# Bias tiles with buffers of their own, loaded in an earlier feed-forward instead of in attention

## The chip, the cores and the metric

The kernel runs on one core of a Trainium2 chip. The metric is the device time of one execution in microseconds (us); the runs of a kernel are given by their median. The profile is of one execution on that core. Its engines are PE (matrix products; PEld is its weight load), DVE (vector), ACT (activations and copies), POOL (a slower vector engine) and SP, whose queue issues the DMAs of this kernel. Each engine works through its own queue in order and waits for others by semaphores.

## The reference

Two layers over 256 positions of width 1024, in float32. A layer is a half-step SwiGLU feed-forward, a mixer, and another half-step feed-forward, each behind an RMS norm. Layer 0's mixer is a gated short convolution; layer 1's is a sparse attention with 16 heads in 4 groups, whose keys and values were computed from layer 0's output.

```python
for i in range(DEPTH):
    if i == N_A_LAYERS:
        kv = shared_kv(h, kv_norm, w_kv, k_norm, ...)
    h = h + 0.5 * swiglu_ffn(rmsnorm(h, ffn1_norm[i]), ffn1_w_in[i], ffn1_w_out[i])
    hn = rmsnorm(h, mix_norm[i])
    if i < N_A_LAYERS:
        h = h + short_conv_mixer(hn, conv_w_in[i], conv_w[i], conv_w_out[i])
    else:
        h = h + nsa_mixer(hn, attn_w_q[j], attn_q_norm[j], attn_w_o[j], rel_bias, kv)
    h = h + 0.5 * swiglu_ffn(rmsnorm(h, ffn2_norm[i]), ffn2_w_in[i], ffn2_w_out[i])
...
def head_bias(rel):                      # added to the scores of every branch of the attention
    return rel_bias[rel_bucket(rel)].reshape(rel.shape + (G, HG)).transpose(2, 3, 0, 1)
```

What matters here is the last piece: the bias of a score depends on the head and on the distance of query and key alone, through a table of 32 buckets.

## The kernel before, in words

The residual stream stays in SBUF, transposed (`hall`: 8 tiles of 128 features x 256 positions). Every product is made in split precision: a float32 operand becomes a rounded high part and a low part, and PE multiplies high by high and low, and low by high. Weights come from HBM through one stream `W`. A DMA brings a chunk of 128 x 2048 into one of three `ws` buffers. A chunk is two units of 1024 columns. `W.high()` makes the high half `wh` of a unit on ACT (L145), `W.low()` the low half `wl` on DVE (L162); there are six buffers of each. The DMA of a chunk waits until DVE has read the chunk that had its `ws` buffer before, three chunks earlier. The chunk of the gate weights is narrower and goes through L140 and L157.

A feed-forward (`ffn_in`) takes 22 steps of 16 + 16 matmuls (L321, L324). After each, ACT and DVE evaluate the previous step's gate and prepare the next units, and a function `bg(f)` may add work at step f. In layer 0's second feed-forward there is none.

The bias of the attention is made once: `tables()`, run at the start of that feed-forward, forms for every head a row of minus the bias by distance and writes the 16 rows to a buffer `row_d` in HBM (L259). A bias tile `bias[j]` of 128 x 2 x 256 holds, for two heads, the row shifted by one element per partition. It is read back from `row_d` by a DMA with overlapping rows (`load_bias`, L818). There are eight, one for each j. On POOL, `c_bias` copies every sixteenth column of a tile into `cbias`, for the compressed branch (L823, L824).

Attention is written out as a list of words (`ORDER`) that is worked through from left to right, each word adding instructions to the queues of one or more engines. The words that matter: `LB_j` loads a bias tile and `CBI_j` copies from it; `WA_u` and `WD_u` are one `W.high()` and one `W.low()`; `F` is six matmuls of the later queries (L900 to L902); `qs`, `qr`, `root`, `recip`, `qn` are the norm of the first queries (ACT L838, DVE L843 and L847, ACT L850, DVE L854 and L873); `GT`, `GC`, `GA`, `GX`, `GE`, `GD` are the gates (PE L915, ACT L920, DVE L923, PE L928, ACT L934, DVE L938 on); `QT` and `QC` transpose the queries and apply their gain (PE L884, ACT L888); `S_j` are the scores of heads j (PE L956), `M` their minima with the bias added (DVE L964; L968 for the compressed branch, from `cbias`), `E` the exponentials (ACT L975), `R` the reciprocals (DVE L979), `N` the scaling (on POOL L990 and L993). Ahead of the list four bias tiles are loaded, and the first queries' product (`b_full`, L584 to L586) is made, with the sums of squares in its middle (`q_mid`, L831). The tiles `act` are a ring of 22 buffers of 128 x 512, used for the feed-forward's hidden tiles, for the bias tiles, and for the attention's transposed queries, weights and outputs. A bias load waits until the last reader of its `act` buffer is done.

Of the kernel before, what the change touches and what calls it, by code (L numbers as in the profile page):

```python
# [9 lines left out]
F32 = mybir.dt.float32  # L10
# [6 lines left out]
P = 128  # L17
# [8 lines left out]
OHW = 512  # L26
# [11 lines left out]


ORDER = """  # L40
CBI_0 GT WA_0 CBI_3 CBI_1 LB_7 qs_0 LB_5 WD_0 LB_4 LB_6 CBI_2 qs_1 F GC qr_0 WA_1 F qr_1 F GA F root exp recip qn_0 GX
F qn_1 GE WD_1 QT_0 QT_1 QC_0 F GD QC_1 S_0 F M_0_1 F F M_0_0 SQ_2 F E_0_1 CBI_4 RD_2 S_1 CBI_5 CBI_7 NW_2 E_0_0 CBI_6
F F F WA_2 QM_2 F R_0_0 WA_3 R_0_1 N_0_0 M_1_1 QT_2 F QC_2 F M_1_0 E_1_1 N_0_1 T_0_0 CM_0 S_2 C_0_0_d SQ_3 R_1_1 WD_2
E_1_0 N_1_1 T_0_1 M_2_1 H_0 CH_0 R_1_0 E_2_1 M_2_0 CX_0 T_1_1 N_1_0 RD_3 S_3 E_2_0 R_2_1 NW_3 N_2_1 T_1_0 CE_0 C_1_1
C_0_1 H_1 M_3_1 C_1_0 CH_1 T_2_1 C_2_1 R_2_0 M_3_0 N_2_0 E_3_1 CR_0 S_4 CM_1 QM_3 E_3_0 CG_0 R_3_1 WD_3 T_2_0 N_3_1
H_2 QT_3 CI_0 M_4_0 QC_3 C_2_0 R_3_0 CL_0 M_4_1 T_3_1 E_4_0 CX_1 CP_0 N_3_0 CPC_0_d S_5 CE_1 R_4_0 E_4_1 CR_1 C_3_1_d
V_1 CG_1 M_5_0 N_4_0 CI_1 CH_2 T_3_0 R_4_1 M_5_1 E_5_0 V_0 CL_1 CM_2 C_3_0_d N_4_1 E_5_1 T_4_0 R_5_0 S_6 C_4_0_d O_0
R_5_1 CP_1 O_1 CX_2 P_0 T_4_1 N_5_0 P_1 CE_2 H_4 CPC_1 CR_2 H_3 M_6_0 CH_4 V_2 CH_3 C_4_1 M_6_1 CG_2 E_6_0 V_3 N_5_1
CI_2 S_7 R_6_0 O_2 O_3 CL_2 P_2 E_6_1 N_6_0 P_3 CP_2 M_7_1 T_5_1 T_5_0 CPC_2 H_5 C_5_1_d C_5_0 V_4 R_6_1 CH_5_d E_7_1
N_6_1 M_7_0 T_6_0 V_5 O_4 R_7_1 CM_3 E_7_0 P_4 CX_3 N_7_1_d WO_0_a O_5 C_6_0 R_7_0 P_5 N_7_0 WA_4 WO_1_a WA_5 WD_4  # L50
T_6_1 CE_3 WD_5 T_7_0 C_6_1 H_6 C_7_0 WO_2_a CH_6_d CR_3 CG_3 WO_3_a CI_3 CL_3 CP_3 T_7_1 CPC_3 H_7 C_7_1_d V_6 CH_7
V_7 O_6 P_6 WO_1_b O_7 P_7 WO_3_b WO_0_b WO_2_b WO_2_c WO_0_c WO_3_c WO_1_c
"""


# [1 line left out]
def trunk(ctx, tc, A, out):  # L57
    nc = tc.nc
    ve, ac, pe, po, sy = nc.vector, nc.scalar, nc.tensor, nc.gpsimd, nc.sync
# [9 lines left out]
    def mk(shape, tag, bufs, dt=F32, pool=None):  # L69
        uid[0] += 1  # L70
        return (pool or sb).tile(list(shape), dt, tag=tag, name=f"{tag}_{uid[0]}", bufs=bufs)

    def one(shape, name, dt=F32):
        return cp.tile(list(shape), dt, tag=name, name=name)
# [4 lines left out]
    def bank2():  # L79
        return mk([P, 2, 512], "mm", 2, pool=ps)  # L80

    def act(shape=(P, 512), dt=F32R):
        return mk(shape, "act", 22, dt)
# [161 lines left out]
    row_d = dr.tile([16, OHW], F32, tag="row", name="row_d")  # L245
# [16 lines left out]
    def new_xs():  # L262
        return [mk([P, 512], "xs", 8, F32R) for _ in range(8)]
# [66 lines left out]
    def total(o, n):  # L330

        r = t2([P, n, T])
        ac.copy(r, o[:, :, T:])  # L333
        ve.tensor_tensor(out=r, in0=o[:, :, :T], in1=r, op=ALU.add)  # L334
        return r
# [4 lines left out]
    def weave(gen):  # L340
        for _ in gen:
            W.pump(1)
        W.pump()

    def ffn_evac(r, R, hid):
        times(r, R, 2)
        yield
        s = t1()
        ac.activation(s, r[:, 0], AF.Silu)  # L349
        ve.tensor_tensor(out=s, in0=s, in1=r[:, 1], op=ALU.mult)  # L350
        yield
        hd = act()
        split(s, hd)
        hid.append(hd)

    def a_group(parts, xs, mid=None):
        us = W.take(len(parts))
        if mid is None:
            a_pass([(o, u, xs, range(8)) for o, u in zip(parts, us)])
        else:  # L360
            a_pass([(o, u, xs, range(6)) for o, u in zip(parts, us)])
            a_pass([(o, u, xs, [6]) for o, u in zip(parts, us)])
            mid()
            a_pass([(o, u, xs, [7]) for o, u in zip(parts, us)])
        W.done(len(parts), False)

    def ffn_in(xs, norm, R=None, bg=None, pre=None, sums=(), rms=None):

        hid, sums = [], list(sums)
        box = [R]  # L370
        n0 = len(sums)

        def mid():
            if pre is not None:
                pre()
            box[0] = norm.rows()

        for f in range(n0, NF):
            o = bank2()
            if f == n0 and n0:  # L380
                box[0] = rms(o)
            else:
                a_group([o[:, 0], o[:, 1]], xs, mid if f == 0 and R is None else None)
            sums.append(total(o, 2))
            for _ in range(2 if len(sums) > 1 else 1):
                weave(ffn_evac(sums.pop(0), box[0], hid))
            if bg is not None:
                bg(f)
        return hid
# [55 lines left out]
    xs = new_xs()  # L445
    nm = Norm([(xs, G_FFN1)])
# [69 lines left out]
    hid = ffn_in(xs, nm, sums=first_tiles(), rms=first_rms)  # L516
    xs = new_xs()
    nm = Norm([(xs, G_MIX)])
# [39 lines left out]
    xs = new_xs()  # L558
    nm = Norm([(xs, G_FFN2)])
    tab = tables()  # L560
    next(tab)
    out_proj(zs, 1.0, nm)
    hid = ffn_in(xs, nm, pre=lambda: list(tab))


    xs = new_xs()
    xk_a = mk([P, 4, 512], "kt", 1, F32R)
    xkv = [xk_a[:, k] for k in range(4)] + [t2(dt=F32R) for _ in range(4)]
    nm = Norm([(xkv, G_KV), (xs, G_FFN1 + 8)])
# [72 lines left out]
    for tt in range(2):  # L642
        for x in range(2):
            src = oc[tt][:, x * 256:(x + 1) * 256].rearrange("p (a d) -> p a d", d=64)
# [115 lines left out]
    def bg(f):  # L760

        if f == 0:
            kv["s"] = squares(kns)
        elif f == 1:
            r = inv_rms(kv["s"])
            for tt in range(2):
                v = kns[tt].rearrange("p (n d) -> p n d", d=64)
                po.tensor_tensor(out=v, in0=v, in1=r[:, tt * 8:tt * 8 + 8, None].to_broadcast([P, 8, 64]), op=ALU.mult)
        elif f in (2, 3, 4, 5):
            c_trans((f - 2) % 2, (f - 2) // 2)  # L770
        elif f in (6, 7):
            k_trans(f - 6)
        elif f == 8:
            po.tensor_tensor(out=both, in0=ident[:, :64], in1=ident[:, 64:], op=ALU.add)
            po.tensor_tensor(out=both48, in0=ident[:96, :48], in1=ident[:96, 48:96], op=ALU.add)
        elif f == 9:
            kv["rk"] = rh_split(0)
        elif f == W1AT[0]:
            kv["ak"] = c_hidden(kv["rk"])
        elif f == 12:  # L780
            kv["ak"] = c_total(kv["ak"])
            kv["rv"] = rh_split(1)
            W.limit = NBUF
        elif f == W1AT[1]:
            kv["av"] = c_hidden(kv["rv"])
            kv["kc"] = kc_norm(c_second(kv["ak"], 0))
        elif f == 15:
            kv["av"] = c_total(kv["av"])
        elif f == 16:
            kc_trans(kv["kc"])  # L790
        elif f == 17:
            c_values(kv["av"])

    hid = ffn_in(xs, None, R1, bg)
    xs = new_xs()
    nm = Norm([(xs, G_MIX + 8)])
# [4 lines left out]
    G = one([P, 2, 48], "G")  # L801


    cbias = one([P, 8, 2, 2, 16], "cbias")
    po.memset(cbias.rearrange("p a b c d -> p (a b c d)"), 1e32)
    cs = [one([P, 8, 4, 16], f"cs{x}", F32R) for x in range(2)]
    for x in range(2):
        po.memset(cs[x].bitcast(F32).rearrange("p a b c -> p (a b c)"), 0.0)
    ac.activation(mk([P, 1], "warm", 1), epst, AF.Sqrt)
    W.cap = W.at + 9  # L810
    bias, qt, ct, oT, wo, wo_banks, X = {}, {}, {}, [], [], [], {}

    def load_bias(j):
        pp, hg = divmod(j, 4)
        b = act([P, 2, 256], F32)
        src = bass.AP(tensor=row_d.tensor, offset=row_d.offset + (8 * pp + hg) * OHW,
                      ap=[[1, P], [4 * OHW, 2], [1, 256]])
        sy.dma_start(b, src)  # L818
        bias[j] = b

    def c_bias(j):
        t = bias[j][:, :, ::-1]
        po.tensor_copy(out=cbias[:, j, 0, :, :7], in_=t[:, :, 159:256:16])  # L823
        po.tensor_copy(out=cbias[:, j, 1, :, :15], in_=t[:, :, 31:256:16])  # L824

    def q_mid():
        pb = bank()
# [255 lines left out]
    def wo_part(c, part):  # L1085
# [12 lines left out]
        "SQ": lambda q: [q_square(q, tt, T) for tt in range(2)], "RD": lambda q: [q_reduce(q, tt, T) for tt in range(2)],  # L1098
        "NW": q_newton, "QM": lambda q: [q_normed(q, tt, T) for tt in range(2)], "QT": q_trans, "QC": q_gain,
        "F": lambda: next(lq), "GT": g_sum, "GC": g_copy, "GA": g_total, "GX": g_trans, "GE": g_exp, "GD": g_out,  # L1100
        "LB": load_bias, "CBI": c_bias, "S": scores, "M": minima, "E": exps, "R": recip,
        "N": lambda j, g, e="": normed(j, g, ve if e else po), "T": trans, "H": trans_hi,
        "C": lambda j, g, e="": copied(("t", j, g), mk([P, 2, T], "xs", 8), copy[e]),
        "CH": lambda j, e="": copied(("t", j), act([P, 2, 2, P], F32), copy[e]),
# [3 lines left out]
        "WA": lambda u: W.high(), "WD": lambda u: W.low(), "WO": wo_part,  # L1108
    }

    for j in range(4):
        load_bias(j)
    om = bank2()
    X["o", 0] = b_full(xs, q_mid, None, [om[:, 0], om[:, 1]])
    del om
# [5 lines left out]
    xs = new_xs()  # L1121
    nm = Norm([(xs, G_FFN2 + 8)])
# [22 lines left out]
    hid = ffn_in(xs, nm)  # L1145
# [77 lines left out]
```

## Time and profile before

| | us |
|---|---|
| median of 3 runs | 997.87 (997.70 to 999.05) |
| span of the profiled execution | 996.8 |
| median less that span | 1.07 |
| PE busy in the span | 977.8 (98%) |
| DVE / ACT / POOL busy | 734.2 / 563.2 / 160.8 |
| q1, the queue of SP's DMAs | 176.66 MB, 51.9% of 16 engines |

For the profiled execution the profile gives its span, from the first to the last instruction; the time of that execution is taken as the span, and the median of the runs as 1.07 us above it. In the rows, an instruction has its start in us, its duration in us, engine, line, operation, output <- input, shapes and count; a bracket gives the idle time of the engine before it and what ended it. Matmuls overlap, so that their durations add up to more than the time they take. "PEclk" is the granted clock of PE, 1.00 being full; "DMA share" is the busy share of the 16 DMA engines. For DMAs, a row gives size and time from issue to landing.

### The profile page before, as it was taken

Reading aid. Unit: us, or ns where it says so; the run is one execution under the profiler, and the core shown is the slowest. Engines: PE = TensorE matmul, PEld = TensorE weight load, DVE = VectorE, ACT = ScalarE, POOL = GpSimd, SP = SyncE. Lnnn points to the kernel's source line nnn. Section 1 sums busy time; section 2 is a strip of 40 time slices with the busy share of each in tenths; the row PEclk is TensorE's granted clock in tenths of the full one; section 3 lists DMA queues with packets and bytes.
Section 4 is the critical chain, followed back from the end, with each engine's and each line's share of the span. In section 5 each row is a group of like instructions: output and inputs, shape, how many; then the busy total and the mean of one; then the engine's idle time right before and its main releaser. Section 6 shows DMA issues by size and latency. Waiting matters only on the chain. (4 is left out here: it accounts for less than half of the span.)

```text
span 996.8 us, 14723 instructions
## 1 busy us (share of the span) xinstructions
PE 977.8 (98%) x5682; PEld 851.8 (85%) x5682; DVE 734.2 (74%) x1155; ACT 563.2 (56%) x935; POOL 160.8 (16%) x256
## 2 busy tenths in 40 slices
PE   9999999999999999999999999999889999999998
PEld 7888888888888888888888898888767878888887
DVE  6888776578898777676569988855587598787652
ACT  7666553455556565644556667643488466565530
POOL 0000001245450000011111121011248340000000
PEclk9999999999999999999999999999998999999999
DMA  8565555545646555645634566654711146555550
GB/s 301 173 226 188 188 192 180 202 167 172 220 169 210 175 200 178 211 169 182 204 135 161 205 213 216 211 201 140 252 45 43 43 169 211 189 191 187 199 185 22
DMA packets 29441, 177.59 MB, mean 178 GB/s; under 512 B 3339, under 2 KB 7179, under 8 KB 8764
## 3 DMA queue, kind: packets, MB, share of 16 engines
q1 hardware_dynamic: 29372, 176.66, 51.9%
q8 instruction: 44, 0.72, 0.3%
q14 instruction: 25, 0.20, 0.1%
HBM read 175.57 MB, written 1.08 MB: 177 GB/s over the span
## 5 line engine op out<-in xcount | busy, mean ns | idle before, releaser
L162 DVE TENSOR_TENSOR wl<-ws,wh 128x1024 fp32r<-128x1024 f32 x320 | 394.3, 1246 | 105.6 <-PE a L424 61.6
L321 PE MATMUL mm<-xs,wh 128*128 128x512 f32 x1488 | 359.6, 393 | 3.2 <-DVE xs L277 2.1
L145 ACT CAST wh<-ws 128x1024 fp32r<-128x1024 f32 x320 | 330.8, 1046 | 47.5 <-PE a L422 21.7
L321 PEld LDWEIGHTS mm<-xs,wh 128*128 128x128 f32 x1488 | 273.7, 189 | 57.4 <-DVE xs L277 2.8
L324 PEld LDWEIGHTS mm<-xs,wl 128*128 128x128 f32 x1488 | 192.2, 192 | 7.9
L324 PE MATMUL mm<-xs,wl 128*128 128x256 f32 x1488 | 194.4, 283 | 0.0
L422 PE MATMUL a<-act,wh 128*128 128x512 f32 x722 | 171.6, 391 | 1.3 <-DVE act L328 1.3
L422 PEld LDWEIGHTS a<-act,wh 128*128 128x128 f32 x722 | 133.3, 188 | 29.1 <-DVE act L328 3.0
L334 DVE TENSOR_TENSOR t<-mm,t 128x512 f32<-128x512 f32 x96 | 66.1, 688 | 74.1 <-ACT t L333 73.4
L333 ACT COPY t<-mm 128x512 f32<-128x512 f32 x96 | 56.1, 585 | 97.7 <-PE mm L324 95.1
L424 PEld LDWEIGHTS a<-act,wl 128*128 128x128 f32 x722 | 91.4, 191 | 2.7
L424 PE MATMUL a<-act,wl 128*128 128x256 f32 x722 | 92.3, 283 | 0.0
L273 ACT ACTIVATE xs<-hall,gains 128x256 fp32r<-128x256 f32 x48 | 24.0, 506 | 92.0 <-DVE hall L393 79.1
L349 ACT ACTIVATE t<-t 128x256 f32<-128x256 f32 x88 | 36.8, 418 | 63.1 <-DVE t L338 63.0
L338 DVE TENSOR_TENSOR t<-t,R 128x512 f32<-128x512 f32 x88 | 61.7, 701 | 2.9
L327 ACT CAST act<-t 128x256 fp32r<-128x256 f32 x96 | 39.0, 407 | 29.1 <-DVE t L539 19.2
L288 POOL TENSOR_TENSOR sq<-hall 128x256 f32<-128x256 f32 x5 | 3.1, 613 | 319.3 <-DVE hall L393 308.7
L291 POOL TENSOR_TENSOR t<-hall 128x256 f32<-128x256 f32 x35 | 27.1, 774 | 134.6 <-DVE hall L393 114.3
L328 DVE TENSOR_TENSOR act<-t,act 128x256 fp32r<-128x256 f32 x96 | 40.9, 426 | 4.7 <-ACT act L327 4.7
L277 DVE SCALAR_TENSOR_TENSOR xs<-hall,gains,xs 128x256 fp32r<-128x256 f32 x48 | 29.1, 614 | 15.6 <-ACT xs L273 15.6
L350 DVE TENSOR_TENSOR t<-t,t 128x256 f32<-128x256 f32 x88 | 37.0, 421 | 3.4 <-ACT t L349 3.3
L393 DVE SCALAR_TENSOR_TENSOR hall<-a,hall 128x256 f32<-128x256 f32 x78 | 32.9, 421 | 7.9 <-PE a L424 5.8
(246 smaller groups left out, 842.0 us busy)
## 6 DMA issues: line engine op xcount, KB each, us to landing
ws<-in_ffn_w_in_dram SPq DMA_DIRECT2D x85, 1024.0 KB, 4.9
ws<-in_ffn_w_out_dram SPq DMA_DIRECT2D x44, 1024.0 KB, 4.8
ws<-in_conv_w_in_dram SPq DMA_DIRECT2D x12, 1024.0 KB, 4.7
ws<-in_w_kv_dram SPq DMA_DIRECT2D x6, 1024.0 KB, 4.9
ws<-in_conv_w_out_dram SPq DMA_DIRECT2D x4, 1024.0 KB, 4.9
ws<-in_attn_w_q_dram SPq DMA_DIRECT2D x4, 1024.0 KB, 4.9
ws<-in_attn_w_o_dram SPq DMA_DIRECT2D x4, 1024.0 KB, 12.5
act<-row_d SPq DMA_DIRECT2D x8, 256.0 KB, 11.0
```

Source lines behind the costliest of these rows:

```text
L145: ac.copy(h, src)
L162: ve.tensor_tensor(out=l, in0=src, in1=h.bitcast(F32), op=ALU.subtract)
L321: pe.matmul(o, u[0][:, k * P:(k + 1) * P], xs[k], start=(k == 0), stop=False)
L324: pe.matmul(o[:, :T], u[1][:, k * P:(k + 1) * P], xs[k][:, :T], start=False, stop=(k == last))
L327: ac.copy(dst[:, :T], src)
L328: ve.tensor_tensor(out=dst[:, T:], in0=src, in1=dst[:, :T].bitcast(F32), op=ALU.subtract)
L333: ac.copy(r, o[:, :, T:])
L334: ve.tensor_tensor(out=r, in0=o[:, :, :T], in1=r, op=ALU.add)
L338: ve.tensor_tensor(out=r, in0=r, in1=R[:, None, :].to_broadcast([P, n, T]), op=ALU.mult)
L350: ve.tensor_tensor(out=s, in0=s, in1=r[:, 1], op=ALU.mult)
L422: pe.matmul(o, wh, lhs[k], start=(k == 0), stop=False)
L424: pe.matmul(o[:, :T], wl, lhs[k][:, :T], start=False, stop=(k == n - 1))
```

## The change

The eight bias tiles become tiles of their own, `bias0` to `bias7`, 2 KB per partition each, and no longer take `act` buffers; the DMA scratch is set to 512 bytes, which leaves their space. `cbias` is set up ahead of layer 0's second feed-forward. One tile is loaded after each of its steps 4 to 11, and one is copied from after each of its steps 13 to 20. The words `LB` and `CBI` leave `ORDER`; the other words stay in their order.

```diff
-CBI_0 GT WA_0 CBI_3 CBI_1 LB_7 qs_0 LB_5 WD_0 LB_4 LB_6 CBI_2 qs_1 F GC qr_0 WA_1 F qr_1 F GA F root exp recip qn_0 GX
+GT WA_0 qs_0 WD_0 qs_1 F GC qr_0 WA_1 F qr_1 F GA F root exp recip qn_0 GX F qn_1 GE WD_1 QT_0 QT_1 QC_0 F GD QC_1 S_0
...
-    hid = ffn_in(xs, nm, pre=lambda: list(tab))
+    bias = {}
+    cbias = one([P, 8, 2, 2, 16], "cbias")
+    po.memset(cbias.rearrange("p a b c d -> p (a b c d)"), 1e32)
+
+    def load_bias(j):
+        pp, hg = divmod(j, 4)
+        b = one([P, 2, 256], f"bias{j}")
+        src = bass.AP(tensor=row_d.tensor, offset=row_d.offset + (8 * pp + hg) * OHW,
+                      ap=[[1, P], [4 * OHW, 2], [1, 256]])
+        sy.dma_start(b, src)
+        bias[j] = b
+
+    def c_bias(j):
+        t = bias[j][:, :, ::-1]
+        po.tensor_copy(out=cbias[:, j, 0, :, :7], in_=t[:, :, 159:256:16])
+        po.tensor_copy(out=cbias[:, j, 1, :, :15], in_=t[:, :, 31:256:16])
+
+    def bias_bg(f):
+
+        if 4 <= f < 12:
+            load_bias(f - 4)
+        elif 13 <= f < 21:
+            c_bias(f - 13)
+
+    hid = ffn_in(xs, nm, pre=lambda: list(tab), bg=bias_bg)
...
-    cbias = one([P, 8, 2, 2, 16], "cbias")
-    po.memset(cbias.rearrange("p a b c d -> p (a b c d)"), 1e32)
...
-    def load_bias(j):
-        pp, hg = divmod(j, 4)
-        b = act([P, 2, 256], F32)
...
-    for j in range(4):
-        load_bias(j)
...
-    nc = _bacc.Bacc("TRN2", target_bir_lowering=False, num_devices=1)
+    nc = _bacc.Bacc("TRN2", target_bir_lowering=False, num_devices=1, dynamic_dma_scratch_size=512)
```

How this moves the instructions is seen on SP and POOL. First SP's queue at the start of attention, before: `row_d` is the source of the bias loads, and the numbers tell tiles of one name apart.

```order
L118 DMA ws_6699<-in_attn_w_q_dram 128x2048
L818 DMA act_6730<-row_d 128x2x256
L818 DMA act_6732<-row_d 128x2x256
L818 DMA act_6734<-row_d 128x2x256
L818 DMA act_6736<-row_d 128x2x256
L118 DMA ws_6753<-in_attn_w_o_dram 128x2048
L118 DMA ws_6787<-in_attn_w_o_dram 128x2048
L818 DMA act_6826<-row_d 128x2x256
L818 DMA act_6830<-row_d 128x2x256
L818 DMA act_6834<-row_d 128x2x256
L818 DMA act_6836<-row_d 128x2x256
L118 DMA ws_6854<-in_attn_w_o_dram 128x2048
```

And the same place in the changed kernel:

```order
L117 DMA ws_6719<-in_attn_w_q_dram 128x2048
L117 DMA ws_6733<-in_attn_w_q_dram 128x2048
L117 DMA ws_6777<-in_attn_w_o_dram 128x2048
L117 DMA ws_6811<-in_attn_w_o_dram 128x2048
L117 DMA ws_6862<-in_attn_w_o_dram 128x2048
```

The four bias loads between attn_w_q and the first chunk of attn_w_o are gone, and the four ahead of its third chunk.

They stand now in SP's queue in layer 0's second feed-forward, which had only weights there; the changed kernel from step 4 on:

```order
L117 DMA ws_3108<-in_ffn_w_in_dram 128x2048
L571 DMA bias_3115<-row_d 128x2x256
L117 DMA ws_3163<-in_ffn_w_in_dram 128x2048
L571 DMA bias_3170<-row_d 128x2x256
L117 DMA ws_3218<-in_ffn_w_in_dram 128x2048
L571 DMA bias_3225<-row_d 128x2x256
```

Each follows the weight load of its step; all eight go in this way.

On POOL, before, the copies stood at the start of attention, between the set-up of the compressed branch's tiles `cs`, the gates' scale (L930) and the first scaling of the heads (L990):

```order
L808 MEMSET cs_6725 128x512
L823 COPY cbias<-act_6730 128x2x7
L824 COPY cbias<-act_6730 128x2x15
L823 COPY cbias<-act_6736 128x2x7
L824 COPY cbias<-act_6736 128x2x15
...
L930 TENSOR_SCALAR sm_6888<-sm_6881 128x2
L823 COPY cbias<-act_6834 128x2x7
L824 COPY cbias<-act_6834 128x2x15
...
L990 TENSOR_TENSOR sm_7014<-sm_7014,G 128x4
```

In the changed kernel nothing is left between them:

```order
L829 MEMSET cs_6757 128x512
L936 TENSOR_SCALAR sm_6896<-sm_6889 128x2
L996 TENSOR_TENSOR sm_7016<-sm_7016,G 128x4
L999 TENSOR_TENSOR pr_6968<-pr_6968,sm_7016 128x128 x2
L999 TENSOR_TENSOR pr_6968<-pr_6968,sm_7016 128x256 x2
```

The copies are now in the feed-forward, where POOL had no work. The order of PE, ACT and DVE is the same as before in both kernels.

More of the change, by code (lines that the diff above doesn't have):

```diff
@@ L40 @@
 ORDER = """
-CBI_0 GT WA_0 CBI_3 CBI_1 LB_7 qs_0 LB_5 WD_0 LB_4 LB_6 CBI_2 qs_1 F GC qr_0 WA_1 F qr_1 F GA F root exp recip qn_0 GX
[L42 to L50, printed above, removed]
@@ L51 @@
-T_6_1 CE_3 WD_5 T_7_0 C_6_1 H_6 C_7_0 WO_2_a CH_6_d CR_3 CG_3 WO_3_a CI_3 CL_3 CP_3 T_7_1 CPC_3 H_7 C_7_1_d V_6 CH_7
-V_7 O_6 P_6 WO_1_b O_7 P_7 WO_3_b WO_0_b WO_2_b WO_2_c WO_0_c WO_3_c WO_1_c
+GT WA_0 qs_0 WD_0 qs_1 F GC qr_0 WA_1 F qr_1 F GA F root exp recip qn_0 GX F qn_1 GE WD_1 QT_0 QT_1 QC_0 F GD QC_1 S_0
+F M_0_1 F F M_0_0 SQ_2 F E_0_1 RD_2 S_1 NW_2 E_0_0 F F F WA_2 QM_2 F R_0_0 WA_3 R_0_1 N_0_0 M_1_1 QT_2 F QC_2 F M_1_0
+E_1_1 N_0_1 T_0_0 CM_0 S_2 C_0_0_d SQ_3 R_1_1 WD_2 E_1_0 N_1_1 T_0_1 M_2_1 H_0 CH_0 R_1_0 E_2_1 M_2_0 CX_0 T_1_1 N_1_0
@@ new lines @@
+RD_3 S_3 E_2_0 R_2_1 NW_3 N_2_1 T_1_0 CE_0 C_1_1 C_0_1 H_1 M_3_1 C_1_0 CH_1 T_2_1 C_2_1 R_2_0 M_3_0 N_2_0 E_3_1 CR_0
+S_4 CM_1 QM_3 E_3_0 CG_0 R_3_1 WD_3 T_2_0 N_3_1 H_2 QT_3 CI_0 M_4_0 QC_3 C_2_0 R_3_0 CL_0 M_4_1 T_3_1 E_4_0 CX_1 CP_0
+N_3_0 CPC_0_d S_5 CE_1 R_4_0 E_4_1 CR_1 C_3_1_d V_1 CG_1 M_5_0 N_4_0 CI_1 CH_2 T_3_0 R_4_1 M_5_1 E_5_0 V_0 CL_1 CM_2
+C_3_0_d N_4_1 E_5_1 T_4_0 R_5_0 S_6 C_4_0_d O_0 R_5_1 CP_1 O_1 CX_2 P_0 T_4_1 N_5_0 P_1 CE_2 H_4 CPC_1 CR_2 H_3 M_6_0
+CH_4 V_2 CH_3 C_4_1 M_6_1 CG_2 E_6_0 V_3 N_5_1 CI_2 S_7 R_6_0 O_2 O_3 CL_2 P_2 E_6_1 N_6_0 P_3 CP_2 M_7_1 T_5_1 T_5_0
@@ L53 @@
+CPC_2 H_5 C_5_1_d C_5_0 V_4 R_6_1 CH_5_d E_7_1 N_6_1 M_7_0 T_6_0 V_5 O_4 R_7_1 CM_3 E_7_0 P_4 CX_3 N_7_1_d WO_0_a O_5
+C_6_0 R_7_0 P_5 N_7_0 WA_4 WO_1_a WA_5 WD_4 T_6_1 CE_3 WD_5 T_7_0 C_6_1 H_6 C_7_0 WO_2_a CH_6_d CR_3 CG_3 WO_3_a CI_3
+CL_3 CP_3 T_7_1 CPC_3 H_7 C_7_1_d V_6 CH_7 V_7 O_6 P_6 WO_1_b O_7 P_7 WO_3_b WO_0_b WO_2_b WO_2_c WO_0_c WO_3_c WO_1_c
 """
@@ L810, in trunk @@
     W.cap = W.at + 9
-    bias, qt, ct, oT, wo, wo_banks, X = {}, {}, {}, [], [], [], {}
-    def load_bias(j):
-        pp, hg = divmod(j, 4)
-        b = act([P, 2, 256], F32)
[L816 to L824, printed above, removed]
+    qt, ct, oT, wo, wo_banks, X = {}, {}, [], [], [], {}
     def q_mid():
@@ L1100, in trunk @@
         "F": lambda: next(lq), "GT": g_sum, "GC": g_copy, "GA": g_total, "GX": g_trans, "GE": g_exp, "GD": g_out,
-        "LB": load_bias, "CBI": c_bias, "S": scores, "M": minima, "E": exps, "R": recip,
+        "S": scores, "M": minima, "E": exps, "R": recip,
         "N": lambda j, g, e="": normed(j, g, ve if e else po), "T": trans, "H": trans_hi,
```

## The prediction

> **What bounds the kernel now.** I began with the busy time by stretches, to find which engine paces the two places the diff touches: layer 0's second feed-forward (about 290 to 400 us) and the start of attention (700 to 730 us).
>
> ```profile
> core 0: us, PE busy (x) PEld busy (x) DVE busy (x) ACT busy (x) POOL busy (x), PEclk, DMA share, GB/s
> 312.50:390.00 77.50, 77.50 (x448) 68.54 (x447) 60.89 (x85) 45.95 (x71) 0.00 (x0) 1.00 0.58 194
> 715.24:719.41 4.17, 0.00 (x1) 0.00 (x1) 3.06 (x7) 3.55 (x7) 0.00 (x0) 1.00 0.81 308
> 719.41:723.10 3.69, 3.69 (x19) 3.69 (x19) 3.59 (x7) 2.06 (x5) 2.13 (x9) 0.54 0.26 85
> ```
>
> In the feed-forward PE is busy throughout at full clock, while POOL is empty and DMA is 58% busy. In attention PE stands still from 715.24 to 719.41 and runs the next 3.69 us at 0.54 of its clock. What a microsecond is worth differs, then: in the feed-forward only a new PE wait costs time, in attention an existing PE wait can go. The timelines of PE and DVE say what PE waits for.
>
> ```profile
> 710.36 2.02 PE L915 MATMUL a<-xs,wh 128*96 128x512 f32 x8
> 714.96 0.28 PE L902 MATMUL a<-wl,xs 128*128 128x256 f32 x1
> 719.41 1.08 PE L928 MATMUL a<-both,t 96*128 96x48 f32 x4 [4.17 <-DVE t L923]
> 721.71 1.60 PE L884 MATMUL a<-small,t 128*128 128x128 f32 x8
> 723.95 1.65 PE L956 MATMUL mm<-kt,act 64*128 64x288 f32 x12
> ...
> 716.35 1.23 DVE L162 TENSOR_TENSOR wl<-ws,wh 128x1024 fp32r<-128x1024 f32 x1 [6.60 <-ACT wh L145]
> 718.94 0.41 DVE L923 TENSOR_TENSOR t<-a,t 96x256 f32<-96x256 f32 x1
> 719.62 1.29 DVE L873 TENSOR_TENSOR t<-mm,sm 128x512 f32<-128x512 f32 x2
> 725.64 0.29 DVE L964 CUSTOM_DVE_ANT_0 pr<-act,mm 128x128 f32<-128x128 f32 x1 [2.41 <-PE mm L956]
> ```
>
> L928 (step GX) needs L923 (GA). GA ran as soon as DVE reached it, but DVE had itself stood 6.60 us behind L162 (WD_0), which needed ACT's cast WA_0. So the next view is ACT and the SP queue.
>
> ```profile
> 707.17 1.05 ACT L145 CAST wh<-ws 128x1024 fp32r<-128x1024 f32 x1 [1.68 <-PE mm L585]
> 715.27 1.04 ACT L145 CAST wh<-ws 128x1024 fp32r<-128x1024 f32 x1 [7.05 <-DMA ws<-in_attn_w_o_dram]
> 717.19 0.36 ACT L920 COPY t<-a 96x256 f32<-96x256 f32 x1
> ...
> 698.56 0.33 SPq L118 DMA_DIRECT2D ws<-in_attn_w_q_dram  x1
> 698.94 2.29 SPq L818 DMA_DIRECT2D act<-row_d  x4
> 701.33 1.13 SPq L118 DMA_DIRECT2D ws<-in_attn_w_o_dram  x1
> ...
> ws<-in_attn_w_o_dram SPq DMA_DIRECT2D x1, 1024.0 KB, 13.8
> ...
> ws<-in_attn_w_q_dram SPq DMA_DIRECT2D x4, 1024.0 KB, 4.9
> act<-row_d SPq DMA_DIRECT2D x8, 256.0 KB, 11.0
> ```
>
> This is the cause. The first chunk of attn_w_o was issued at 701.33, behind four bias loads, and landed 13.8 us later at 715.13, where the chunks of attn_w_q take 4.9. ACT reached WA_0 after its cast of 707.17 and stood there 7.05 us. Behind WA_0 on ACT are the squares of the queries and the gate copy (L920), behind WD_0 on DVE are their sums and GA, and PE waits for GA. All of this hangs on one weight chunk that DMA traffic made late.
>
> **The change, term by term.**
>
> *Attention, DMAs removed.* SP loses eight L818 issues; attn_w_o follows attn_w_q at once. Its first chunk reuses the ws buffer of the gate weights, whose last reader is the DVE row below. So it issues at 699.00 instead of 701.33.
>
> ```profile
> 698.45 0.55 DVE L157 TENSOR_TENSOR wh<-ws,wh 128x384 fp32r<-128x384 f32 x1
> ...
> DMA to landing us min/median/max: 4.8/4.9/7.2
> 709.89 0.39 PE L585 MATMUL mm<-wh,xs 128*128 128x512 f32 x1
> ```
>
> Landing lies between 4.9 (alone) and 13.8 (with all the bias traffic). The slowest weight chunk of the feed-forward stretch took 7.2, and here too only one other chunk is in flight, so I take 7.2: landed at 706.2. ACT then no longer waits for DMA. What it waits for next is a wh buffer: there are six, WA_0's was last read by the L585 above, and the earlier cast at 707.17 shows the same kind of wait. That L585 ends at 710.28, so WA_0 starts at 710.37 instead of 715.27, 4.9 us earlier, with 4 us to spare on the DMA.
>
> *What follows it.* The squares need the query product, which ends one matmul after that L585, and follow the cast. The gate copy needs L915, which ends at 712.38, so it runs near 712.4; 717.19 less 4.9 would be 712.29, hence no more than 0.1 is lost, off DVE's path. GA, 718.94 to 719.35, moves to about 714.04 to 714.45. PE finishes L902 at 715.24. GA is ready 0.8 us ahead, and the wait of 4.17 us goes whole. Next in line is L884 (QT), which needs L873, done at 720.91 less 4.9 = 716.0; PE gets there at 715.24 + (721.71 - 719.41) x 0.54 = 716.5. Then S_0's L956 needs ACT's gain of the queries, which by the same sums is done about when PE arrives: at most 0.1 us to pay.
>
> *The clock.* The 3.69 us after the wait ran at 0.54. With no idle stretch before it I take full clock, 3.69 x 0.54 = 2.0 us, so 1.7 us more go. The bounds are 0 (the clock falls anyway) and 1.7; the full clock is nearer, since the feed-forward row, with PE full throughout, shows 1.00.
>
> *Does the shift survive attention?* DVE idles 2.41 us before its first minima (L964 at 725.64), waiting for S_0. It comes 4.9 us earlier and S_0 5.9, so about 1.4 us of this idle time is left and S_0 still sets the start. ACT and POOL are in the same position:
>
> ```profile
> 727.25 0.66 ACT L838 ACTIVATE t<-a 128x256 f32<-128x256 f32 x2 [3.18 <-PE a L902]
> 732.24 0.20 POOL L990 TENSOR_TENSOR sm<-sm,G 128x4 f32<-128x4 f32 x1 [9.97 <-DVE sm L979]
> ```
>
> Nothing in the heads' loop had begun before S_0, so all three engines move with it.
>
> *POOL in attention.* A memset, sixteen small copies and their DMA waits leave the queue. POOL idled 9.97 us there, so this is worth nothing.
>
> *Feed-forward, eight loads added.* Each bias load goes to SP right behind a weight load. SP mostly waits there, so issuing is free. The DMA work is priced from the stretch in which only such small packets moved:
>
> ```profile
> DMA packets 436, 0.43 MB, mean 142 GB/s; under 512 B 21, under 2 KB 436, under 8 KB 436
> 703.00:706.00 3.00, 3.00 (x14) 2.47 (x14) 1.70 (x2) 2.04 (x3) 0.10 (x1) 1.00 0.88 142
> ...
> 314.44 0.33 SPq L118 DMA_DIRECT2D ws<-in_ffn_w_in_dram  x1
> 320.01 0.33 SPq L118 DMA_DIRECT2D ws<-in_ffn_w_in_dram  x1
> 318.75 1.23 DVE L162 TENSOR_TENSOR wl<-ws,wh 128x1024 fp32r<-128x1024 f32 x1
> 331.93 0.59 ACT L333 COPY t<-mm 128x512 f32<-128x512 f32 x1 [1.62 <-PE mm L324]
> ```
>
> There 0.43 MB kept all engines busy for 0.88 x 3 us, so a tile of 0.26 MB is 1.6 us of all sixteen. A step is 320.01 - 314.44 = 5.57 us with 0.58 x 5.57 = 3.2 us of transfers, and 3.2 + 1.6 = 4.8 fits. If it does delay a weight chunk, there is room: the chunk issued at 320.01 takes the buffer freed at 319.98, two chunks already loaded are cast in the next two steps, and its own cast follows the copy (L333) of 331.93, near 332.4. That is 12.4 us after the issue, against a landing of 4.9. Cost 0; the upper end is 8 x 1.6 = 12.8 us if nothing covers it.
>
> *Feed-forward, POOL copies added.* Two per step, for eight steps:
>
> ```profile
> 720.47 0.20 POOL L823 COPY cbias<-act 128x14 f32<-128x14 f32 x1
> 720.61 0.23 POOL L824 COPY cbias<-act 128x30 f32<-128x30 f32 x1
> 721.32 0.79 POOL L823 COPY cbias<-act 128x14 f32<-128x14 f32 x1 [0.47 <-DMA act<-row_d]
> 720.82 1.22 DVE L162 TENSOR_TENSOR wl<-ws,wh 128x1024 fp32r<-128x1024 f32 x1
> ```
>
> A copy of 0.20 us took 0.79 while DVE's L162 ran, and L162 kept its usual 1.22: POOL waited, not DVE. Were DVE held up instead, it would lose 0.20 + 0.23 per step out of (77.50 - 60.89) / 77.50 x 5.57 = 1.2 us idle. Cost 0, bounds 0 and 8 x 0.43 = 3.4 us. The Trainium skill (SBUF — State Buffer, section on the two separate sides) says that VectorE operations with two SBUF inputs and GpSimd operations that read SBUF exclude each other on a shared port pair, and that the loser blocks fully; that speaks against putting the copies beside a busy VectorE. The 0.79 us copy agrees with it, but the engine blocked was the idle one. By that rule the sum could be up to 3.4 us worse, by the rows it is not.
>
> *Buffers and scratch.* Bias tiles no longer take act buffers; the later users of those waited for nothing long. The smaller scratch removes no instruction. Cost 0, bounded by the 0.2% that a measurement tells.
>
> **Sum.** 4.17 + 1.7 = 5.9 us (5.87). The profiled execution's span of 996.8 becomes 990.9. The median of the runs, 997.87, lies 1.07 above that span, and I keep this offset: 992.0 us.
>
> **Rivals.** *The chunk still comes late.* If it took 13.8 us from 699.00 it would land at 712.8 instead of 715.13, a gain of 2.3 on the path, and 1.8 us of the wait would stay. With the clock kept that makes 997.87 - 2.3 - 1.7 = 993.9, without it 995.5. For: the chunk is the second of two in flight. Against: what slowed it is what leaves, and the wait returns only when the landing passes 12.1 us (711.1, with GA's 0.8 us of room).
>
> *The clock falls elsewhere, or not at all.* Attention has a second, unrelated stall:
>
> ```profile
> 743.00:746.70 3.70, 1.42 (x8) 0.87 (x8) 3.46 (x19) 3.21 (x10) 1.32 (x3) 1.00 0.00 0
> 746.70:752.70 6.00, 5.94 (x20) 4.33 (x21) 5.96 (x36) 2.98 (x13) 5.68 (x13) 0.50 0.22 53
> 746.76 4.26 PE L956 MATMUL mm<-kt,act 64*128 64x288 f32 x12 [2.06 <-DVE sm L979]
> ```
>
> PE was 38% busy for 3.7 us, and then had half its clock for 6.0. The same twelve matmuls took 1.65 at 723.95 and 4.26 here. A stall that comes 6 us earlier may or may not be followed by such a fall; if it is not, up to 2.6 us more go: 989.4. The Trainium skill (TensorE: Matmul & The Clock Gate, "What's actually happening") says that the gate watches a free-running window of about 3.4 us, halves the clock after an idle window and restores it after a busy one. Both stalls here agree in their 0.5 and the first in its 3.69 us; that the window is not tied to the program cannot be seen in one trace, but it is the reason to give this rival a chance of its own.
>
> *The gain is given back.* The heads' loop is paced by DVE, ACT and POOL rather than PE, so a PE stall ahead of it could be slack: 997 to 998. Against: the three idle rows above, each released by PE or by what PE released.
>
> *Slower.* Bias loads delay weights in the feed-forward, where PE has no cover. Price 8 x 1.6 = 12.8 less the 5.9: 1004.8. It decides once a chunk lands over 12.4 us after its issue; 7.2 + 1.6 = 8.8 is far from that. For it: bias loads took 11.0 us and the weight chunk among them 13.8, but with several bias loads outstanding instead of one.
>
> **Chances.** The sum as it stands 0.66 (990.9 to 993.2 of its own), late chunk 0.12, clock luck 0.10, given back 0.07, slower 0.05. The first three make 0.88; the range reaches from 989.8, near the clock's case, to 995.0, within the late chunk's. A measurement here can tell about 0.2%, 2 us, from no change: below 995.87 is faster, 0.87; same 0.08; slower 0.05.
>
> **What would show it.** Right: the attn_w_o chunk issued about 2.3 us sooner relative to the last attn_w_q and landed in under 9 us; WA_0 released by PE, not by DMA; no wait of PE before GX; full clock through the gates and S_0; no ACT cast waiting for DMA in the feed-forward, with bias loads landing inside a step or two. Wrong: a DMA wait of WA_0 that stays, a new PE wait at QT or S_0, a longer stall among the heads, or casts in the feed-forward that wait for weights.

## The result, and the profile after

The changed kernel took 991.99 us (median of four runs, 989.48 to 992.91) against 998.20 us for the kernel before in the same comparison: a ratio of 0.9932, 95% interval 0.9917 to 0.9948. Repeated later with more runs it gave 992.08 us and 0.9942 (0.9929 to 0.9956). The forecast was 992.0. The span of the profiled execution went from 996.8 to 990.4 us.

First the busy time by stretches, after: the feed-forward that took in the loads, the stretch of attention from GX to S_0 (before, 719.41 to 723.95 with a clock of 0.62), and the second stall of the heads.

```profile
312.50:390.00 77.50, 77.50 (x448) 68.51 (x447) 60.86 (x85) 45.93 (x71) 5.19 (x16) 1.00 0.69 221
714.84:717.68 2.84, 2.84 (x26) 2.71 (x24) 2.81 (x5) 2.22 (x6) 0.00 (x0) 1.00 0.02 6
742.00:748.00 6.00, 6.00 (x26) 4.97 (x24) 4.47 (x24) 1.87 (x6) 5.77 (x14) 0.50 0.48 172
```

PE is still full in the feed-forward (77.50 of 77.50), with DMA at 0.69 instead of 0.58. From GX to S_0 it takes 2.84 us at full clock instead of 4.54. The later fall to half clock is still there. Then the rows of PE, ACT, DVE and SP that answer to those shown of before; GX is now L934, S_0 L962, GA L929 and the minima L970.

```profile
714.72 0.28 PE L908 MATMUL a<-wl,xs 128*128 128x256 f32 x1
714.84 0.54 PE L934 MATMUL a<-both,t 96*128 96x48 f32 x4
716.01 1.04 PE L890 MATMUL a<-small,t 128*128 128x128 f32 x8
717.68 1.65 PE L962 MATMUL mm<-kt,act 64*128 64x288 f32 x12
...
710.12 1.05 ACT L144 CAST wh<-ws 128x1024 fp32r<-128x1024 f32 x1 [2.14 <-PE mm L608]
713.80 0.41 DVE L929 TENSOR_TENSOR t<-a,t 96x256 f32<-96x256 f32 x1
719.38 0.29 DVE L970 CUSTOM_DVE_ANT_0 pr<-bias,mm 128x128 f32<-128x128 f32 x1 [1.30 <-PE mm L962]
...
698.79 0.34 SPq L117 DMA_DIRECT2D ws<-in_attn_w_o_dram  x1
DMA to landing us min/median/max: 4.6/4.8/4.8
704.50:705.00 0.50, 0.50 (x4) 0.42 (x3) 0.50 (x1) 0.50 (x1) 0.00 (x0) 1.00 0.67 279
705.20:705.40 0.20, 0.20 (x3) 0.16 (x2) 0.12 (x1) 0.05 (x1) 0.00 (x0) 1.00 0.01 0
```

The first attn_w_o chunk goes out at 698.79. The trace has no landing for it; the row of landings is that of the three later chunks, 4.6 to 4.8 us. But only the last attn_w_q chunk and this one are in flight then, and the last two rows show their transfers ending at about 705.0, 6.2 us after the issue. WA_0 starts at 710.12, released by PE. GA is done at 714.21, and L934 follows L908 without a wait.

### The profile page after: what moved, and what is told of

Its sections match the earlier page's. It is cut to its first block, busy times and chain, and to the rows that moved or that the text cites. A ratio compares the mean times of both kernels' runs of the same rounds, so it can differ in the third digit from the quotient of the medians.

```text
span 990.4 us, 14708 instructions
## 1 busy us (share of the span) xinstructions
PE 976.1 (99%) x5682; PEld 850.7 (86%) x5682; DVE 734.1 (74%) x1155; ACT 563.4 (57%) x935; POOL 162.3 (16%) x256
## 5 line engine op out<-in xcount | busy, mean ns | idle before, releaser
L161 DVE TENSOR_TENSOR wl<-ws,wh 128x1024 fp32r<-128x1024 f32 x320 | 394.1, 1246 | 100.7 <-PE a L423 61.6
L349 DVE TENSOR_TENSOR t<-t,t 128x256 f32<-128x256 f32 x88 | 37.0, 421 | 3.4 <-ACT t L348 3.3
```

What stands on the lines that cost most here:

```text
L161: ve.tensor_tensor(out=l, in0=src, in1=h.bitcast(F32), op=ALU.subtract)
```

## The experiments

The question was which part of the change carries the gain: the buffers, the copies, the absence of the loads from attention, or only their place in SP's queue. The theory was the last: what counts is that bias loads stood ahead of one weight chunk. Two more runs look for the price of the loads in the feed-forward, two for the clock.

### own_bufs: buffers alone

```diff
-        b = act([P, 2, 256], F32)
+        b = one([P, 2, 256], f"bias{j}")
...
+    nc = _bacc.Bacc("TRN2", target_bir_lowering=False, num_devices=1, dynamic_dma_scratch_size=512)
```

> The kernel before, with one part of the change: the bias tiles have buffers of their own (and the smaller scratch), but are loaded and copied in attention as before. My theory (the first attn_w_o chunk lands late because bias loads stand ahead of it and share the DMA engines) expects the stall to stay: that chunk lands 12 to 14 us after its issue, WA_0 waits for it, PE waits 3 to 4.5 us ahead of GX, time 996.5 to 999. The rival that the buffers did it (bias loads that waited for act buffers blocked the queue) expects the wait gone and about 992.

Measured: 998.12 us, ratio 0.9997 (0.9986 to 1.0007). The waits of PE and ACT around the gates, from its table of waits (engine, line, waited for: total, times, longest):

```profile
PE a L928 <- DVE t L923: 4.3, 1, 4.3
ACT wh L145 <- DMA ws<-in_attn_w_o_dram: 7.2, 1, 7.2
```

Both are as before (4.17 and 7.05). Buffers of their own and the smaller scratch are worth nothing by themselves.

### copies_attn: the copies stay in attention

```diff
-        elif 13 <= f < 21:
-            c_bias(f - 13)
```

In the order written out for attention, CBI_0 to CBI_7 stand again where the kernel before had them, with LB left out.

> The changed kernel, but the sixteen POOL copies into cbias (and only they) are back in attention, where the kernel before had them; the loads stay in the feed-forward. My theory expects the changed kernel's time, 991 to 993, no PE wait ahead of GX, and POOL idle over 8 us before its first scaling of the heads. The rival that POOL's work in attention cost time expects 994 or more.

Measured: 991.44 us, ratio 0.9932 (0.9919 to 0.9945). The changed kernel's time, with the copies back. POOL's part of the change is worth nothing either.

### dummy_2, dummy_3, dummy_first, dummy_second: loads put back into attention

The first three put two, three and four extra loads ahead of the first attn_w_o chunk of the changed kernel; the last puts four behind the second chunk.

```diff
+    for j in range(4):          # 2 in dummy_2, 3 in dummy_3
+        dummy_load(j)           # act([P, 2, 256]) <- row_d, as load_bias before
     om = bank2()
```

> The changed kernel, with four extra bias loads (into act buffers, read by nothing) where the first four stood before, between attn_w_q and the first attn_w_o chunk. If the DMA engines work in the order of issue, the four cost 4 x 1.6 = 6.4 us behind attn_w_q (landed 703) and ahead of 2.6 us of the chunk: landed at about 712, PE waits about 1 us ahead of GX, time 992.5 to 994. If loads issued later share the engines with the chunk (the second four were in flight too in the kernel before, which landed it at 715.1), the chunk still lands near 712 here, since the second four are absent. If the first four alone explain all: landed at 715, stall 4 us, clock fall, 997 to 999. Rival that traffic is not the cause: 992.

> The changed kernel, with four extra bias loads (into act buffers, read by nothing) where the second four stood before, behind the second attn_w_o chunk. The first chunk has landed by about 704 to 706, before these are issued, so my theory expects no PE wait ahead of GX and the changed kernel's time, 991 to 993. Rival (any bias traffic around the gates delays something there, as by slowing SP's queue or the second chunk): over 994.

> The changed kernel with two extra bias loads (read by nothing) between attn_w_q and the first attn_w_o chunk. With none that chunk lands about 705, with four 715.4, so about 2.6 us per load: two should land it near 710, just about when ACT can start WA_0 (710.1) and before the point (711.1) from which I predicted a PE wait ahead of GX. Expected: no wait or under 0.5 us, 991.5 to 993. If any load ahead of the chunk brings the stall back: 995 or more.

> The same with three extra loads. By the same step the chunk lands near 712.5: past the point, so PE waits about 1.5 us ahead of GX, and the rest depends on the clock: 993.5 if it stays full, 995 if it falls after so short a wait. If the wait grows with every load from the first: about 996.5.

| loads ahead of the chunk | WA_0 starts | PE waits ahead of GX | time, us | ratio (interval) |
|---|---|---|---|---|
| 0 (changed kernel, repeated) | 710.12 (first profile) | 0 | 992.08 | 0.9942 (0.9929 to 0.9956) |
| 0, four behind the second chunk | 710.21 | 0 | 992.48 | 0.9943 (0.9931 to 0.9955) |
| 2 | 711.13 | none shown (see below) | 992.15 | 0.9951 (0.9937 to 0.9965) |
| 3 | 713.23 | 2.33 | 995.91 | 0.9982 (0.9971 to 0.9992) |
| 4 | 715.54 | 4.44 | 998.35 | 1.0001 (0.9993 to 1.0010) |

The timelines with two, three and four loads, in this order: ACT's cast WA_0 and PE's GX; then, with three, the stretches around the wait.

```profile
711.13 1.05 ACT L144 CAST wh<-ws 128x1024 fp32r<-128x1024 f32 x1 [2.97 <-DMA ws<-in_attn_w_o_dram]
715.28 0.65 PE L941 MATMUL a<-both,t 96*128 96x48 f32 x4
```

```profile
713.23 1.05 ACT L144 CAST wh<-ws 128x1024 fp32r<-128x1024 f32 x1 [5.21 <-DMA ws<-in_attn_w_o_dram]
717.37 1.09 PE L941 MATMUL a<-both,t 96*128 96x48 f32 x4 [2.33 <-DVE t L936]
714.70:717.10 2.40, 0.34 (x3) 0.14 (x2) 2.40 (x6) 1.83 (x5) 0.00 (x0) 0.97 0.49 208
717.10:722.70 5.60, 5.33 (x24) 5.20 (x24) 3.97 (x8) 3.38 (x7) 0.22 (x1) 0.50 0.32 85
```

```profile
715.54 1.04 ACT L144 CAST wh<-ws 128x1024 fp32r<-128x1024 f32 x1 [7.33 <-DMA ws<-in_attn_w_o_dram]
719.68 1.09 PE L941 MATMUL a<-both,t 96*128 96x48 f32 x4 [4.44 <-DVE t L936]
...
ws<-in_attn_w_o_dram SPq DMA_DIRECT2D x1, 1024.0 KB, 14.0
```

Four loads that nothing reads bring back the whole stall and the whole time. Four loads behind the second chunk bring back nothing. The chunk lands at about 705.0 without loads ahead of it, at 711.0 with two, 713.1 with three and 715.4 with four: about 6 us for the first two together, then 2.1 and 2.3 us each. Most of what the first two cost is hidden, because ACT can't start WA_0 before 710.1 in any case. With two, ACT waits for the DMA, and GX starts 0.37 us behind the last matmul of `F` instead of 0.12: the cast at 711.13 is just about what GA's room covers. Past it lateness becomes PE wait nearly one to one: WA_0 2.10 us later for the first 2.33 us of wait, another 2.31 for another 2.11.

For four loads I had expected a chunk landed near 712 and under 994 us, from 1.6 us a load and transfers in the order of issue. It landed 14.0 us after its issue, at 715.4. Whether the loads take longer or the second chunk shares the engines with the first (issued at about 705) stays open: the DMA rows here give the engines' mean, not the slowest. The next run speaks against the second, for there what is issued behind the chunk does not hold it up.

### wo_first_1: the order of the queue alone

The kernel before, with its first four bias loads issued inside `b_full`, behind the first attn_w_o chunk:

```diff
-    for j in range(4):
-        load_bias(j)
     om = bank2()
-    X["o", 0] = b_full(xs, q_mid, None, [om[:, 0], om[:, 1]])
+    X["o", 0] = b_full(xs, q_mid, lambda k: [load_bias(j) for j in range(4)] if k == 1 else None, [om[:, 0], om[:, 1]])
```

> The kernel before, in which only the place of the first four bias loads in SP's queue is different: they are issued behind the first attn_w_o chunk instead of ahead of it. Buffers, copies and the second four are as before. My theory (the place in the queue ahead of that one chunk is all that counts) expects the chunk to land at 704 to 706, no PE wait ahead of GX, and 991 to 993.5, so that moving the loads to the feed-forward was not needed for the gain. Rival: bias loads in attention also share the engines with the chunk when issued right behind it, so that it lands after 711 and the time is 995 to 998; or the heads then wait for their bias tiles, over 994, seen as DVE waiting for row_d's loads at its first minima.

Measured: 992.06 us, ratio 0.9947 (0.9932 to 0.9962). Its timelines of SP, ACT, POOL and PE, and two stretches of DMA:

```profile
698.82 0.33 SPq L118 DMA_DIRECT2D ws<-in_attn_w_o_dram  x1
699.21 2.26 SPq L818 DMA_DIRECT2D act<-row_d  x4
...
710.15 1.05 ACT L145 CAST wh<-ws 128x1024 fp32r<-128x1024 f32 x1 [2.14 <-PE mm L585]
717.12 0.49 ACT L934 ACTIVATE G<-a,sm 128x48 f32<-128x48 f32 x2 [1.43 <-POOL sm L930]
714.91 0.20 POOL L823 COPY cbias<-act 128x14 f32<-128x14 f32 x1 [5.41 <-DMA act<-row_d]
715.89 1.19 POOL L930 TENSOR_SCALAR sm<-sm 128x2 f32<-128x2 f32 x1
718.24 1.65 PE L956 MATMUL mm<-kt,act 64*128 64x288 f32 x12 [0.46 <-ACT act L888]
...
704.00:705.00 1.00, 1.00 (x6) 0.84 (x5) 1.00 (x1) 0.77 (x1) 0.00 (x0) 1.00 0.94 395
706.00:707.00 1.00, 1.00 (x6) 0.81 (x5) 0.54 (x1) 0.04 (x1) 0.00 (x0) 1.00 0.60 57
```

The chunk leaves 0.4 us ahead of the loads instead of behind them, WA_0 is released by PE, and the whole gain is there with all eight loads still in attention. The DMA runs at the rate of weights until 705 (395 GB/s) and only then falls to that of the loads (57), so the four loads right behind the chunk did not hold it up. What is left is a wait of 0.46 us at S_0, which the time doesn't tell from nothing. It comes through POOL: the gates' scale L930 stands behind copies that wait until 714.91 for a bias tile and then takes 1.19 us (0.22 before) while DVE's L162 runs; ACT's L934 waits 1.43 us for it, and the gain of the queries (L888) follows. Taking loads and copies out of attention removes this too.

### ffn_2x, ffn_4x: the price of the loads in the feed-forward

```diff
         if 4 <= f < 12:
+            for _ in range(3):      # 1 in ffn_2x
+                spare_load(f - 4)   # a buffer of attention's <- row_d, read by nothing
             load_bias(f - 4)
```

> The changed kernel with four bias loads instead of one in each of the eight feed-forward steps (the extra three into buffers that attention uses later, read by nothing). It looks for the point of my slower rival. A step of 5.57 us then has 3.2 us of weight transfers and four loads of 1.1 us (from the rise of the DMA share, 0.58 to 0.69, in the changed kernel) to 1.6 us (my price), 7.6 to 9.6 us: 2 to 4 us too much per step, 16 to 32 us over eight steps, of which the slack of a chunk (12.4 - 4.8 = 7.6 us) is covered. So ACT's casts wait for weights and the time is 1000 to 1017. If small loads fit beside the weights whatever their number: 992.

> The changed kernel with two bias loads instead of one in each of the eight feed-forward steps (the second into a buffer that attention uses later, read by nothing). Four per step cost 45 us, 1.9 us for each of the 24 extra loads. With two, a step of 5.57 us has 3.2 us of weights and two loads of 1.1 to 1.9 us, 5.4 to 7.0: at most 1.4 us too much per step, 11 us in eight steps, of which 7.6 us are covered by the chunk's slack. Expected 992 to 995.5, with weights landing up to 13 us after issue. If a second load already costs what the further ones did (8 x 1.9): 1007.

Measured: with two loads per step 991.89 us, ratio 0.9942 (0.9926 to 0.9959); with four 1036.91 us, ratio 1.0405 (1.0380 to 1.0430). With two, the feed-forward's stretch and the landing of its weights:

```profile
312.50:390.00 77.50, 77.50 (x447) 68.50 (x447) 61.01 (x84) 46.14 (x71) 7.59 (x16) 1.00 0.85 248
DMA to landing us min/median/max: 4.8/8.0/14.2
```

With four, the waits of ACT and PE from 300 to 450, the feed-forward's stretch, one in which hardly anything but these loads moved, and the landing of weights:

```profile
ACT wh L144 <- DMA ws<-in_ffn_w_in_dram: 62.7, 8, 11.3
PE mm L320 <- DVE t L333: 32.7, 7, 6.7
312.50:390.00 77.50, 60.16 (x306) 51.71 (x305) 37.09 (x53) 27.62 (x43) 1.89 (x10) 0.87 0.94 183
320.00:330.00 10.00, 10.00 (x57) 8.70 (x56) 7.67 (x12) 6.31 (x10) 0.00 (x0) 1.00 0.98 75
DMA to landing us min/median/max: 5.0/17.0/23.4
```

Two per step are covered: PE stays full, though weights land up to 14.2 us after issue, later than the 12.4 from which the prediction saw a cost. Four are not, and cost 45 us, more than the 25 I had allowed: 0.262 MB at 75 GB/s is 3.5 us a load, not 1.1 to 1.6. PE's waits make 32.7 of the 45; the sum had no term for the clock, which fell to 0.87 in the feed-forward's stretch. The cover is real and its end lies between two and four loads a step.

### warm1, warm12: fillers against the later falls of the clock

```diff
-CR_0 S_4 CM_1
+CR_0 Z S_4 CM_1       # Z: 8 x pe.matmul(z[:, 816:944], ones, ones), z a score tile of S_3
...
+        if fill: fill()       # warm12 only: 4 matmuls each, ahead of inputs 6 and 7 of the last ffn_in's first step
```

> The changed kernel with eight extra 128 x 128 matmuls of ones ahead of S_4, into columns 816 to 943 of a score tile that nothing reads. They fill the 2.0 us in which PE waits for DVE there (738.4 to 740.5). My theory of the clock (it falls to half after a stretch with little PE work, and returns after some microseconds of full work) expects no fall after 740 and up to 2.7 us less than the changed kernel, 989 to 990.5; the spread of the changed kernel's runs (989.5 to 992.9, clock 0.998 to 0.994) is then mostly this fall, and shrinks. Rival: the 2.0 us alone do not decide the fall, or the filler delays S_4: 992 or more.

> The same, and in the last feed-forward's first step four such matmuls each ahead of the sixth and seventh input tile, where PE waits about 1 us each (798.9 to 801) and then has half its clock for about 4 us. If both falls go: another 1 to 1.8 us, 987 to 989.5. If the short waits there are not what makes the clock fall: as the kernel with the first filler alone.

> The changed kernel unaltered, beside the kernels with fillers on the same chip: 990 to 992.5, some executions near 989.5 where the clock does not fall after 740.

Measured: 991.77 us (ratio 0.9943, 0.9929 to 0.9957) and 993.50 us (0.9955, 0.9940 to 0.9970), beside 992.08 of the changed kernel. The timeline of the first:

```profile
740.47 2.80 PE L970 MATMUL mm<-ones 128*128 128x128 f32 x16 [1.94 <-DVE t L981]
743.20 2.57 PE L962 MATMUL mm<-kt,act 64*128 64x288 f32 x12
```

The filler didn't run in the wait but after it: it was made to wait for DVE's last reading of the score tiles, as S_4 was, and then held S_4 up until 743.20. So this tells nothing on whether PE work inside the wait would keep the clock, and no version here beats the changed kernel. With the second filler the forecast of 987 to 989.5 was missed: the clock still falls there (0.76 from 800 to 805), and why that kernel is 1.4 us slower than the changed one is not shown. Filling the wait needs a PSUM region that no reader guards; none was free, and it wasn't tried.

## Why the prediction was right, point by point

**The wait of 4.17 us.** Right, in place, cause and size. L928 stood 4.45 us behind the start of L902; L934 stands 0.12 behind L908. That the cause is the loads ahead of the chunk is shown by dummy_first, which restores the wait, and wo_first_1, which removes it without moving the loads out of attention.

**The clock, 1.7 us.** Right in kind, and in size for the two profiled executions: 4.54 us from GX to S_0 became 2.84 at a clock of 1.00, 1.70 less. The size is partly luck, because the stretch at half clock is not the same after the same wait. The same ten microseconds, first before, then in own_bufs, and then own_bufs from GX to S_0:

```profile
716.00:726.00 10.00, 6.59 (x40) 5.95 (x41) 7.14 (x16) 5.84 (x12) 2.13 (x9) 0.83 0.64 232
716.00:726.00 10.00, 6.51 (x34) 6.24 (x36) 6.78 (x13) 6.04 (x12) 2.18 (x9) 0.66 0.67 236
719.49:724.80 5.31, 5.31 (x25) 5.18 (x25) 3.71 (x7) 3.14 (x6) 2.18 (x9) 0.52 0.47 134
```

A mean of 0.83 over 10 us is 3.4 us at half clock, one of 0.66 is 6.8. From GX to S_0 own_bufs took 5.31 us and dummy_first 5.42, so there the clock cost 2.5 and 2.6 us. dummy_3 adds that in its profiled execution a wait of only 2.33 us was followed by 5.6 us at 0.50, so the two terms are not separate: a wait of half the size is paid for in the clock as well (995.91, near the 995.5 of the rival without the clock). Its twelve runs reach from 994.13 to 997.13, with mean clocks of 0.996 to 0.992, so here too the fall differs between executions.

**The sum.** S_0 began 6.27 us earlier. Of this 0.25 was there before anything in attention changed (L915 began at 710.36, now 710.11), and the gate stretch itself gives 4.33 + 1.70 = 6.03 where 5.9 stood. The medians differ by 6.2. One step was mis-sized and hidden: the offset of 1.07 us between the span and the time. The profiled execution after took 992.23 us for a span of 990.4, an offset of 1.83; the 1.07 mixed a median with the span of another execution. With 1.83 the same sum would have said 992.7, so the agreement to 0.01 us is luck; the size of the gain, 5.9 forecast against 6.2 measured, is not taken from the offset.

**What follows.** WA_0 at 710.37 was to be released by PE; less the early 0.25 that is 710.12, and it is 710.12. The landing was taken as 7.2 us, and the transfers ended some 6.2 us after the issue: near enough, with 4 us to spare. DVE's idle time ahead of the minima was to shrink from 2.41 to about 1.4, and is 1.30. S_0 had no wait.

**The feed-forward.** Cost 0 was right, the price behind it was not. From the DMA share, a load costs (0.69 - 0.58) x 77.5 / 8 = 1.1 us where it has one to itself; ahead of the chunk in attention it delays the landing by 2.1 to 3 us, and where only loads queue it takes 3.5. The 1.6 taken from one stretch is none of these. The bias rows, and POOL and DVE beside each other:

```profile
bias<-row_d SPq DMA_DIRECT2D x8, 256.0 KB, 6.2
...
339.21 1.23 DVE L161 TENSOR_TENSOR wl<-ws,wh 128x1024 fp32r<-128x1024 f32 x1
339.30 1.23 POOL L577 COPY cbias<-bias 128x30 f32<-128x30 f32 x1
340.36 0.46 DVE L349 TENSOR_TENSOR t<-t,t 128x256 f32<-128x256 f32 x1
```

The copies ran as soon as a tile had landed (320 to 363 us), not in the steps after which they are written, since POOL had nothing else in its queue. A copy of 0.23 us took 1.23 beside L161, whose 1.23 is its usual time; L349 behind it took 0.46 instead of 0.42. This is what the Trainium skill says (SBUF — State Buffer, the two separate sides): the later one of the two blocks fully. Here that was POOL: the two long copies of the sixteen (1.23 us, and 1.10 at 361.66) both began behind an L161. So the 3.4 us that the rule would allow against the change were not paid.

**The rivals.** The late chunk's point was set at a landing of 711.1; dummy_2, with its cast at 711.13, has none that the trace shows (GX is 0.25 us late), dummy_3, at 713.23, has. The slower rival's mechanism exists, with its point between two and four loads a step. Given back: no, S_0 moved by 6.27 us and the end of the span by 6.4. The clock's luck remains a chance: one of the first four executions had a mean clock of 0.998 instead of 0.994 or 0.995 and a span of 987.7, 2.7 below the profiled one, which is the 2.6 of that rival; but that execution has no trace here, and that the second fall was absent in it is not shown. That this fall varies is: over the 18 us from 739 the mean clock is 0.81 in the profiled execution of the changed kernel and 0.91 in those of dummy_first and warm1, 6.8 against 3.2 us at half clock.

## What to carry to other kernels

When an engine waits for a weight load, look at what stands ahead of that load in its queue: here the order of issue of one DMA against four small ones was worth 0.6%, and the rest of the change nothing that the time can tell. Find the one transfer that work is queued behind, and issue it first; moving the others to a quieter stage is one way to do that, not the only one. Price a transfer where it will run and beside what will run there: the same load was 1.1 us, 2.1 to 3, or 3.5. And a loss of clock behind a wait is not a fixed price: 1.7 us in one trace here, 2.5 and 2.6 in others with nearly the same wait.

## What was not expected of the hardware

The loads with overlapping rows from the 32 KB of `row_d` move little for the engine time that they take: in ffn_4x they kept the 16 engines 98% busy at 75 GB/s, where the weights reach over 400 (434 GB/s from 703 to 704 us in the changed kernel). In the kernel before, a stretch of such packets moved 142 GB/s at 88%. What separates the two figures was not tested.

The clock fell to 0.50 at the end of a PE wait of 2.33 us, with 0.34 us of work in 2.40 (dummy_3). The Trainium skill (TensorE: Matmul & The Clock Gate, "What's actually happening") speaks of an idle window of about 3.4 us; this stretch holds none that is wholly idle and of that length.
